# Experts of a two-block transformer on one core: gate and up as plain float32 matmuls in four column groups over 96 slots, weights unsplit

## The chip, the cores and the metric

The kernel runs on one core of a Trainium2 chip. The metric is the device time of one execution in microseconds, the median of several runs. The engines are TensorE (PE in the profile, with its weight loads as PEld), VectorE (DVE), ScalarE (ACT), GpSimd (POOL) and SyncE (SP, which issues most of the DMAs).

## What is computed

A sequence of 256 tokens with 1024 features passes through two blocks of two layers each, all in float32: mixers, feed-forward layers, and at the very end a layer of eight experts of which each token takes two. Only that last layer is touched here. From the reference:

```python
def swiglu(h, w_gate, w_up, w_down):
    return (jax.nn.silu(h @ w_gate) * (h @ w_up)) @ w_down

def moe_swiglu(h, router, w_gate, w_up, w_down):
    ...
    probs = jax.nn.softmax((ht @ router).astype(F32), axis=-1)
    top_p, top_i = lax.top_k(probs, TOP_K)
    top_p = top_p / jnp.sum(top_p, axis=-1, keepdims=True)
    gates = jnp.sum(jax.nn.one_hot(top_i, N_EXPERTS, dtype=F32) * top_p[..., None], axis=1).astype(h.dtype)
    out = jnp.zeros_like(ht)
    for e in range(N_EXPERTS):
        out = out + gates[:, e:e + 1] * swiglu(ht, w_gate[e], w_up[e], w_down[e])
    return out.reshape(B, T, D)
```

Here there are 8 experts, 2 for each token, 1024 features and 1536 features inside an expert. Gate, up and down of an expert are 6 MB each, 151 MB for the layer.

## The kernel before

**Split products.** Most products of the kernel are made of three. A weight tile W arrives as float32 in a buffer `raw` (`wload`, L294: one DMA on SP's queue, 1 MB). ScalarE copies it to `wh` (L302), VectorE subtracts to get `wl` (L303), both in the type float32r. Activations are split in the same way. `mm3` (L308) then adds three matmuls: high times high (L310), high times low (L311), low times high (L312). There are 3 buffers `raw`, and 5 each of `wh` and `wl` (1024 columns, so half a `raw` each); the experts' stage has 4 more of `raw` (`MORE["mo"]`, L33). Other products, in the mixers, are plain float32 matmuls without a split. L1279 in the hybrid mixer is one of these: it multiplies with 64 stationary columns and writes the lower and the upper half of the partitions in turn.

**The experts' stage** (`moe`, L1375). `first_up` (L1454) does gate and up of the first 512 features of expert 0 for all 256 tokens while the router works; the matmuls begun in `head_rows` at the end of the stage ahead belong to it. `router` and `shares` give each token its two experts, its place in each, and its weight. `experts(base, mid)` (L1477) then treats every expert on at most 128 tokens: those with places `base` to `base + 127`. In it:

- `places` (L1481) makes the one-hot matrices `oh`.
- `gather` (L1490) multiplies x by `oh` for two experts at a time and puts their tokens, features on partitions, into `xg`, split in two parts (L1499 on TensorE, L322 and L324 for the split).
- `up(e, b)` (L1508) makes 512 features of gate and up: 8 row tiles x 2 x 3 products, into the PSUM tag `pj`, then silu and the product `u` (L1523, L1524). There are three such blocks b for an expert.
- `turn` (L1527) transposes `u` (L1548) and splits it into `ph` and `pl`.
- `down` (L1551) multiplies by down's weights into two banks of the tag `sm`; after the third block it turns `oh` (L1568, `ohT` L1570) and splits the result into `yh`, `yl`.
- `scatter` (L1577) multiplies back to the tokens (L1584, L1585) and adds to x (L1586).

The loop at L1599 does `up` of a block, within it the turn and the scatter of earlier ones, then `down` of the block before. A second call, `experts(P, {})`, handles tokens past the 128th of an expert; it stands under a condition on the number of tokens of the fullest expert (L1629 to L1631), and each engine jumps over it when the condition is false. Except where `manual_schedule` is used, a scheduler sets the order of instructions on every engine; for TensorE in `first_up` the written order holds, in `experts` the scheduler's.

## Time and profile before

| | |
|---|---|
| median of 3 runs | 1692.63 us (1692.15 to 1693.01) |
| span of the profiled execution | 1693.5 us |
| TensorE busy in it | 1643.3 us, 97% |
| VectorE busy | 1243.0 us, 73% |
| ScalarE busy | 1025.3 us, 61% |
| moved by DMA | 334.77 MB, mean 198 GB/s |
| first product of the experts to the last down, about | 1257 to 1683 us |

The profile is one execution; the sum of an argument is made against its 1693.5 us, which are 0.9 us above the median. Busy time of TensorE counts pipelined matmuls whose ends are modelled, so the pace of a matmul is read from the starts of successive ones, not from the duration of one.

### The profile page before, as it was taken

The page shows a single profiled execution, that of the slowest core. Times are in us where ns is not written, and L with a number is a line of the kernel's source. Part 1 is how long each engine was busy: PE and PEld are TensorE (multiplying, and loading weights), DVE is VectorE, ACT ScalarE, POOL GpSimd, SP SyncE. Part 2 cuts the span into 40 slices and gives each one's busy share as a digit, 9 for nine tenths or more (in the row PEclk, how much of TensorE's full clock was granted, in tenths as well). Part 3 has the DMA queues.
Part 4 walks back from the last instruction along what each step waited for, and adds up shares of the span by engine and source line. Part 5 has one row for each costly group of instructions (what it writes and reads, how often), then busy time and mean ns, then how long its engine had stood idle before and what let it go on. Part 6 is the DMA issues. An engine that isn't in the chain of part 4 may idle for free.

```text
span 1693.5 us, 25594 instructions
## 1 busy us (share of the span) xinstructions
PE 1643.3 (97%) x9987; PEld 1451.9 (86%) x9987; DVE 1243.0 (73%) x1867; ACT 1025.3 (61%) x1610; POOL 136.0 (8%) x158
## 2 busy tenths in 40 slices
PE   7999999999999999989999999989999999999998
PEld 5878999888889998989899998989778888888886
DVE  6667877666577776886475555875589999999996
ACT  6646555555575555663364444653468777877775
POOL 2100000021000000261000001360000000000000
PEclk9999999999999999999999999999999999999999
DMA  7433555454335553440165554420459899898992
GB/s 279 150 125 127 205 193 180 169 192 167 123 129 198 194 179 137 175 144 1 50 228 195 178 183 156 162 100 1 154 203 362 323 351 353 340 349 327 348 366 111
DMA packets 47376, 334.77 MB, mean 198 GB/s; under 512 B 5424, under 2 KB 5456, under 8 KB 8720
## 3 DMA queue, kind: packets, MB, share of 16 engines
q1 hardware_dynamic: 45936, 327.70, 53.1%
q0 software_dynamic: 736, 4.29, 0.7%
q8 instruction: 80, 1.31, 0.3%
q10 hardware_dynamic: 576, 1.08, 0.2%
q14 instruction: 48, 0.39, 0.1%
HBM read 332.00 MB, written 1.05 MB: 197 GB/s over the span
## 4 chain that ended last, share of the span: by engine, by line
PE 87%; issue 5%; DVE 3%; ACT 2%; POOL 2%; DMA 0%; POOLq 0%; DVEq 0%; ACTq 0%
PE pj L312 18%; PE pj L310 18%; PE pj L311 18%; PE sm L312 7%; PE sm L310 6%; PE sm L311 6%; PE sm L421 2%; PE sm L1147 2%; PE sm L1156 2%; DVE wl L303 1%; PE sm L1150 1%; ACT wh L302 1%; PE sm L1499 1%; POOL qa L1233 1%; PE pj L1255 1%
## 5 line engine op out<-in xcount | busy, mean ns | idle before, releaser
L303 DVE TENSOR_TENSOR wl<-raw,wh 128x1024 fp32r<-128x1024 f32 (+1 forms) x632 | 755.7, 1213 | 208.3 <-ACT wh L302 200.1
L302 ACT CAST wh<-raw 128x1024 fp32r<-128x1024 f32 (+1 forms) x632 | 651.0, 1039 | 293.6 <-PE pj L312 112.6
L310 PE MATMUL pj<-hTh,wh 128*128 128x256 f32 x1192 | 336.1, 282 | 0.0
L311 PE MATMUL pj<-hTl,wh 128*128 128x256 f32 x1192 | 335.8, 282 | 0.0
L312 PE MATMUL pj<-hTh,wl 128*128 128x256 f32 x1192 | 335.3, 282 | 0.0
L310 PEld LDWEIGHTS pj<-hTh,wh 128*128 128x128 f32 x1192 | 227.1, 191 | 1.1
L311 PEld LDWEIGHTS pj<-hTl,wh 128*128 128x128 f32 x1192 | 227.2, 191 | 0.9
L312 PEld LDWEIGHTS pj<-hTh,wl 128*128 128x128 f32 x1192 | 226.8, 191 | 0.2
L311 PE MATMUL sm<-wl,ph 128*128 128x512 f32 x456 | 179.2, 393 | 0.0
L312 PE MATMUL sm<-wh,pl 128*128 128x512 f32 x456 | 177.5, 393 | 0.0
L310 PE MATMUL sm<-wh,ph 128*128 128x512 f32 x456 | 166.4, 393 | 0.5 <-ACT ph L316 0.5
L311 PE MATMUL pj<-wl,xgh 128*128 128x512 f32 x368 | 145.4, 395 | 0.8 <-DVE wl L303 0.8
L312 PE MATMUL pj<-wh,xgl 128*128 128x512 f32 x368 | 143.8, 391 | 0.0
L310 PE MATMUL pj<-wh,xgh 128*128 128x512 f32 x368 | 142.3, 391 | 0.0
L312 PE MATMUL pj<-wh,hTl 128*128 128x512 f32 (+1 forms) x368 | 138.1, 378 | 3.3 <-DVE hTl L324 3.3
L310 PE MATMUL pj<-wh,hTh 128*128 128x512 f32 (+1 forms) x368 | 139.5, 381 | 0.5 <-ACT hTh L322 0.4
L311 PE MATMUL pj<-wl,hTh 128*128 128x512 f32 (+1 forms) x368 | 137.5, 376 | 0.0
L310 PEld LDWEIGHTS sm<-wh,ph 128*128 128x128 f32 x456 | 85.7, 188 | 19.0 <-ACT ph L316 0.7
L312 PEld LDWEIGHTS sm<-wh,pl 128*128 128x128 f32 x456 | 85.5, 188 | 19.1
L311 PEld LDWEIGHTS sm<-wl,ph 128*128 128x128 f32 x456 | 85.6, 188 | 18.5
L832 DVE SCALAR_TENSOR_TENSOR u<-pj,tab_f,u 128x254 f32<-128x254 f32 (+1 forms) x176 | 82.7, 478 | 20.0 <-ACT u L830 18.2
L312 PEld LDWEIGHTS pj<-wh,hTl 128*128 128x128 f32 x368 | 69.5, 189 | 15.7 <-DVE hTl L324 6.1
(402 smaller groups left out, 2411.0 us busy)
## 6 DMA issues: line engine op xcount, KB each, us to landing
raw<-in_mo_u SPq DMA_DIRECT2D x96, 1024.0 KB, 5.2
raw<-in_mo_d SPq DMA_DIRECT2D x48, 1024.0 KB, 5.0
raw<-in_up SPq DMA_DIRECT2D x44, 1024.0 KB, 4.8
raw<-in_dn SPq DMA_DIRECT2D x22, 1024.0 KB, 4.7
raw<-in_fg_u SPq DMA_DIRECT2D x22, 1024.0 KB, 4.8
raw<-in_od_b SPq DMA_DIRECT2D x18, 1024.0 KB, 4.8
raw<-in_hy_b SPq DMA_DIRECT2D x16, 768.0 KB, 4.2
raw<-in_hy_a SPq DMA_DIRECT2D x12, 1024.0 KB, 4.7
```

What stands on the lines that cost most here:

```text
L302: A.copy(h, r)
L303: V.tensor_sub(m, r, h.bitcast(F32))
L310: T.matmul(o, lh, rh, start=first, stop=False)
L311: T.matmul(o, lh, rl, start=False, stop=False)
L312: T.matmul(o, ll, rh, start=False, stop=last)
L421: T.matmul(q, hT[j][:, k, ts_], w[f][k][v], start=t + k + i == 0, stop=k == KT - 1 and i == 2, skip_group_check=True)
L832: V.scalar_tensor_tensor(u[:, g, sh:], q[:, : S - sh], cw[:, f, g, wi : wi + 1], u[:, g, sh:], op0=OP.mult, op1=OP.add)
L1147: T.matmul(pq[:, i * P : (i + 1) * P], Am[:, i], U[:, i], start=i == 0, stop=True, skip_group_check=True)
L1150: T.transpose(pt[:, i * P : (i + 1) * P], U[:, i], ident)
L1156: T.matmul(pu[:, i * P : (i + 1) * P], Tt[:, i], Q[:, i], start=i == 0, stop=True, skip_group_check=True)
L1233: G.tensor_scalar(dst[b, h], C[b], cc[b, h : h + 1], cb[b, h : h + 1], op0=OP.mult, op1=OP.add)
L1255: T.matmul(sc, qa[:, h, ts_], ka[:, h, :w], start=e == 0, stop=False, skip_group_check=True)
```

## The change

Gate and up in `experts` no longer use split products. The gathered tokens `xg` are kept as one float32 tensor, 96 slots for each expert instead of 128, in three tiles of 32 tokens. The weights go from DRAM into seven buffers `mw` of [128, 1536] (768 KB a DMA, gate or up of one row tile) and from there straight into plain float32 matmuls: the tokens are stationary (32 columns), a quarter of the 1536 columns moves in each of four matmuls, and each of the four writes its own group of 32 partitions. Silu, product and transposes work on three tiles of [128, 384]. Down keeps its split products, with 96 stationary columns, over all 1536 features in one go after `up` of the next expert. The PSUM banks are dealt out by hand: six for gate and up and the turns, two for down, gather and scatter. The whole loop now stands under `manual_schedule` for TensorE. Tokens past the 96th and the 192nd of an expert have a conditional pass each, so there are two conditions. `xh` and `xl` move into another pool. The first 512 features of expert 0 come from an array of their own, `mo_h`, as before in content. The diff takes out comments as well, so line numbers after it are other ones.

```diff
-MORE = {"mo": (4, 0), "f": (0, 4), "sw": (0, 4), "ev": (1, 1), "od": (1, 1)}
+MORE = {"mo": (0, 0), "f": (0, 4), "sw": (0, 4), "ev": (1, 1), "od": (1, 1)}
+C32 = 32
+NT = 3
+CAP = C32 * NT
+MW_BUFS = 7
...
-                    def gather(e):
-                        xg[e // 2] = split_pair("xg")
+                    def gather(e, kind="dn"):
+                        xg[e // 2] = xgs[e // 2 % 2]
                         for k0 in range(0, KT, 2):
-                            p = ps()
+                            p = bank(kind)
...
-                            split_gain([(h[:, k0 + k], lo[:, k0 + k], p[:, k * S : (k + 1) * S],
-                                         nrm["g"][:, k0 + k : k0 + k + 1]) for k in range(2)])
+                            for k in (k0, k0 + 1):
+                                src = grp(p[:, (k - k0) * S : (k - k0 + 1) * S], 2)[:, :, :CAP]
+                                A.activation(xg[e // 2][:, k], src, AF.Copy, scale=nrm["g"][:, k : k + 1])
...
-                    def up(e, b):
...
-                                w = unit(e, b, g, half)
-                                for k in range(4):
-                                    kk = half * 4 + k
-                                    mm3(q, h[:, kk, es_], lo[:, kk, es_], *w[k], kk == 0, kk == KT - 1)
...
+                    def up(e):
+                        lo = 512 if e in mid else 0
+                        n = (DE - lo) // 4
+                        h = xg[e // 2]
+                        o = [[bank("up") for _ in range(2)] for _ in range(NT)]
+                        for k in range(KT):
+                            for m in range(2):
+                                w = sp.tile([P, DE], F32, tag="mw", name="mw", bufs=MW_BUFS)
+                                nc.sync.dma_start(w[:, : 4 * n], a["mo_u"][(e * KT + k) * 2 + m][:, lo:])
+                                for t in range(NT):
+                                    l = h[:, k, e % 2, t * C32 : (t + 1) * C32]
+                                    for g in range(4):
+                                        T.matmul(o[t][m][g * C32 : (g + 1) * C32, :n], l, w[:, g * n : (g + 1) * n],
+                                                 start=k == 0, stop=k == KT - 1, skip_group_check=True)
                             yield
+                        made[e] = []
+                        for t in range(NT):
+                            u = sp.tile([P, 384], F32, tag="u", name="u", bufs=4)
+                            A.activation(u[:, :n], o[t][0][:, :n], AF.Silu)
+                            V.tensor_mul(u[:, :n], u[:, :n], o[t][1][:, :n])
+                            made[e].append(u)
...
+                        for t, u in enumerate(made.pop(e)):
+                            p = bank("up")
+                            for i in range(c):
+                                T.transpose(p[:, i * P : (i + 1) * P], u[:, i * P : (i + 1) * P], ident)
+                            part = lambda z: z[:, k1:, t * C32 : (t + 1) * C32].rearrange("p (g c) n -> p c g n", c=c)
+                            split(part(ph), part(pl), p[:, : c * P].rearrange("p (c g n) -> p c g n", c=c, g=4))
...
+                            mm3(acc[n][:CAP], ph[:, kk], pl[:, kk], w[kk][0][:, c], w[kk][1][:, c], kk == 0, kk == nk - 1)
...
+                    for e in range(NE):
+                        side = iter(())
+                        if e >= 2:
+                            side = scatter(e - 2)
+                        if e % 2 == 1 and e + 1 < NE:
+                            side = chain(side, gather(e + 1))
+                        for k, _ in enumerate(up(e)):
+                            if k % 2 == 1:
+                                next(side, 0)
+                                next(side, 0)
+                        rest(side)
+                        if e:
+                            rest(down(e - 1))
+                        turn(e)
+                    last = down(NE - 1)
+                    next(last)
+                    rest(scatter(NE - 2, "up"))
+                    rest(last)
+                    rest(scatter(NE - 1, "up"))
...
-                experts(0, mid)
+                banks["up"] = ([ps("pj") for _ in range(4)] + [ps() for _ in range(2)], 0)
+                banks["dn"] = ([ps() for _ in range(2)], 0)
+                xgs = [xp.tile([P, KT, 2, CAP], F32, tag=tag, name="xg", bufs=2) for tag in ("xTh", "xTl")]
+                with tc.manual_schedule(engines=MAN):
+                    experts(0, mid)
                 full = nc.values_load(mosti[:1, :1], min_val=0, max_val=S)
-                with tc.If(full > P):
-                    experts(P, {})
+                for base in (CAP, 2 * CAP):
+                    with tc.If(full > base):
+                        with tc.manual_schedule(engines=MAN):
+                            experts(base, {})
```

Three places of the order, as it stands before and after. In the rows, a name ahead of the arrow is what is written, those behind it are read, and x4 is a count.

TensorE, in the middle of the stage before, where gather, scatter and `up` of one expert meet (`xgh`, `xgl` are the split tokens, `yh` and `yl` the split result of the expert before):

```order
L1499 MATMUL sm<-oh,xl 128x256
L310 MATMUL pj<-wh,xgh 128x512
L1584 MATMUL sm<-yh,ohT 128x512
L1585 MATMUL sm<-yl,ohT 128x512
L311 MATMUL pj<-wl,xgh 128x512
L312 MATMUL pj<-wh,xgl 128x512
```

After, from the end of down(0) over the turn of expert 1 into up(2) and to its first scatter (L1532 are the matmuls in column groups, 4 of them a bundle):

```order
L316 MATMUL sm<-wh,pl 96x512
L1587 MATMUL pj<-tab_com,oh 96x128 x2
L1566 MATMUL sm<-tab_com,u 128x128 x6
L1566 MATMUL pj<-tab_com,u 128x128 x3
L1532 MATMUL pj<-mw,xg 32x384 x8
L1532 MATMUL sm<-mw,xg 32x384 x4
...
L1532 MATMUL pj<-mw,xg 32x384 x4
L1603 MATMUL sm<-yh,ohT 128x512
L1604 MATMUL sm<-yl,ohT 128x512
```

Single products of gather and scatter stood among those of gate and up; now they stand in blocks between runs of L1532, and down, turn and the next up follow one another.

ScalarE, the same stretch before:

```order
L316 CAST ph<-sm 128x512
L1570 CAST ohT<-sm 128x256
L302 CAST wh<-raw 128x1024 x3
L1523 ACTIVATE u<-pj 128x512
L302 CAST wh<-raw 128x1024 x8
L316 CAST yh<-sm 128x512 x2
L302 CAST wh<-raw 128x1024
```

And after (`ph` comes in three pieces, one for each tile of tokens):

```order
L1538 ACTIVATE u<-sm 128x384
L306 CAST wh<-raw 128x1024 x11
L320 CAST yh<-sm 96x512 x2
L1589 CAST ohT<-pj 96x256
L320 CAST ph<-pj 128x3x4x32 x2
L306 CAST wh<-raw 128x1024
L320 CAST ph<-sm 128x3x4x32
```

The casts of weights are fewer and stand in one block behind the silu; the last piece of `ph` stands behind one more of them. VectorE's order (`yl`, `pl`, `wl`) goes the same way.

SyncE, the loads around the reading of the fullest expert's count (`mosti`), before:

```order
L1629 TENSOR_LOAD mosti
L1629 ISA x2
L297 DMA raw<-in_mo_u 128x2048 x3
L297 DMA raw<-in_mo_d 128x2048 x2
L297 DMA raw<-in_mo_u 128x2048 x4
```

And after:

```order
L1650 TENSOR_LOAD mosti
L1650 ISA x2
L301 DMA raw<-in_mo_d 128x2048 x2
L1528 DMA mw<-in_mo_u 128x1024 x9
L1528 DMA mw<-in_mo_u 128x1536 x23
L301 DMA raw<-in_mo_d 128x2048 x6
L1528 DMA mw<-in_mo_u 128x1536 x16
```

Units of down came after every four of gate and up; now they come six in a row after sixteen pieces, and seven pieces of the next expert's gate and up stand ahead of them.

## Rows read from the trace of the kernel before

**Rows 1.** Page, part 1: engine, busy us, share of the span, instructions

```profile
PE 1643.3 (97%) x9987; PEld 1451.9 (86%) x9987; DVE 1243.0 (73%) x1867; ACT 1025.3 (61%) x1610; POOL 136.0 (8%) x158
```

**Rows 2.** Windows: start:end, busy us PE PEld DVE ACT POOL, clock, DMA, GB/s

```profile
1262.00:1676.00 414.00, 414.00 (x1909) 341.35 (x1907) 385.07 (x388) 325.48 (x368) 0.00 (x0) 1.00 0.88 333
...
1410.00:1420.00 10.00, 10.00 (x45) 8.14 (x45) 9.21 (x9) 8.12 (x9) 0.00 (x0) 1.00 1.00 392
```

**Rows 3.** Waits, 1260 to 1693 us: waiter, releaser, total us, times, longest

```profile
ACT wh L302 <- PE pj L312: 40.9, 99, 2.5
ACT wh L302 <- PE sm L312: 35.2, 72, 2.9
```

**Rows 4.** Groups by form, 1260 to 1693 us: count, busy us, mean ns, idle

```profile
L303 DVE TENSOR_TENSOR wl<-raw,wh 128x1024 fp32r<-128x1024 f32 x275 | 327.2, 1220 | 28.0 <-ACT wh L302 21.9 <-PE pj L312 1.6
L302 ACT CAST wh<-raw 128x1024 fp32r<-128x1024 f32 x275 | 286.5, 1053 | 77.7 <-PE pj L312 40.9 <-PE sm L312 35.2 <-DVE wl L303 1.2
...
L312 PE MATMUL pj<-wh,xgl 128*128 128x512 f32 x367 | 143.3, 391 | 0.0
...
L312 PE MATMUL sm<-wh,pl 128*128 128x512 f32 x192 | 75.5, 395 | 0.0
```

**Rows 5.** Timeline, PE, the first products of two successive gathers: start, us, what

```profile
1325.01 0.28 PE L1499 MATMUL sm<-oh,xh 128*128 128x256 f32 x1
...
1434.88 0.28 PE L1499 MATMUL sm<-oh,xh 128*128 128x256 f32 x1
```

**Rows 6.** Timeline, PE, inside a down, ten products apart

```profile
1398.12 0.39 PE L310 MATMUL sm<-wh,ph 128*128 128x512 f32 x1
...
1400.45 0.40 PE L312 MATMUL sm<-wh,pl 128*128 128x512 f32 x1
```

**Rows 7.** Timeline, PE, the end of the first gather and what follows

```profile
1255.96 0.28 PE L1499 MATMUL sm<-oh,xh 128*128 128x256 f32 x1
...
1256.89 0.39 PE L310 MATMUL pj<-wh,xgh 128*128 128x512 f32 x1
...
1258.56 0.50 PE L311 MATMUL pj<-wl,xgh 128*128 128x512 f32 x1 [0.81 <-DVE wl L303]
```

**Rows 8.** Timeline, PE, plain float32 of 128 columns, and L1279 in two column groups

```profile
788.87 0.83 PE L1147 MATMUL sm<-U,Am 128*128 128x128 f32 x6
789.54 0.49 PE L1150 MATMUL sm<-tab_com,U 128*128 128x128 f32 x3
789.97 0.66 PE L1279 MATMUL pj<-wT,vf 128*64 128x128 f32 x8
790.56 0.70 PE L1255 MATMUL pj<-ka,qa 128*128 128x256 f32 x2
791.10 0.22 PE L1256 MATMUL pj<-causb,identb 128*128 128x128 bf16 x1
```

**Rows 9.** Timeline, PE, plain float32 of 256 columns

```profile
749.09 1.03 PE L1106 MATMUL sm<-C,tab_hy 128*128 128x256 f32 x4
749.96 1.24 PE L1114 MATMUL sm<-kq,kz 128*128 128x256 f32 x5
```

**Rows 10.** Timeline, PE, the last turn and the last down

```profile
1676.67 0.38 PE L1568 MATMUL sm<-tab_com,oh 128*128 128x128 f32 x2
1677.50 0.50 PE L310 MATMUL sm<-wh,ph 128*128 128x512 f32 x1 [0.46 <-ACT ph L316]
```

**Rows 11.** Timeline, DVE, the second product of gate and up

```profile
1256.69 0.68 DVE L1473 TENSOR_TENSOR u<-u,pj 128x512 f32<-128x512 f32 x1
```

**Rows 12.** The line of the condition: count, ns min/median/max, first and last start

```profile
L1630 SPq EVENT_SEMAPHORE  x8: 17/17/17, 1690.1 to 1691.8; - x8
...
L1630 DVEq COMPARE_BRANCH  x1: 72/72/72, 1686.9 to 1686.9; - x1
L1630 SPq COMPARE_BRANCH  x1: 50/50/50, 1687.1 to 1687.1; - x1
...
L1630 DVEq EVENT_SEMAPHORE  x1: 21/21/21, 1690.5 to 1690.5; - x1
```

More of the change, by code (lines that the diff above doesn't have):

```diff
@@ L1458, in first_up @@
                     o[0, 0], o[0, 1] = yield from head
-                    w = [unit(0, 0, 1, half) for half in range(2)]
+                    w = [wload(a["mo_h"][2 + half], 4, 512) for half in range(2)]
                     for t in range(2):
@@ L1474, in first_up, with bank @@
                         split(uh[:, t], ul[:, t], u)
-                    mid[0, 0] = (uh, ul)
+                    mid[0] = (uh, ul)
+                banks = {}
+                def bank(kind):
+                    b, at = banks[kind]
+                    banks[kind] = (b, (at + 1) % len(b))
+                    return b[at]
                 def experts(base, mid):
@@ L1534, in turn @@
+                    def turn(e):
+                        ph = sp.tile([P, DE // P, CAP], F32R, tag="ph", name="ph", bufs=2)
+                        pl = sp.tile([P, DE // P, CAP], F32R, tag="pl", name="pl", bufs=2)
+                        turned[e] = (ph, pl)
+                        k1 = 0
+                        if e in mid:
+                            k1 = 4
+                            u = mid[e]
                             for k0 in (0, 2):
-                                p = ps()
+                                p = bank("up")
@@ L1559, in down @@
+                    def down(e):
+                        ph, pl = turned.pop(e)
+                        acc = [bank("dn"), bank("dn")]
+                        nk = DE // P
+                        w = [None] * nk
+                        steps = [(kk, n) for kk in range(nk) for n in range(2)]
+                        if e == NE - 1:
+                            steps = steps[: 2 * nk - 8] + [(kk, n) for n in range(2) for kk in range(nk - 4, nk)]
                         for kk, n in steps:
                             if w[kk] is None:
-                                w[kk : kk + 2] = wload(a["mo_d"][(e * 3 + b) * 2 + kk // 2], 2, D)
+                                w[kk : kk + 2] = wload(a["mo_d"][e * nk // 2 + kk // 2], 2, D)
@@ L1577, in scatter @@
-                    def scatter(e):
+                            mm3(acc[n][:CAP], ph[:, kk], pl[:, kk], w[kk][0][:, c], w[kk][1][:, c], kk == 0, kk == nk - 1)
+                            if (kk, n) == (3, 1):
+                                yield
+                        p = bank("up")
+                        for t in range(2):
+                            T.transpose(p[:CAP, t * P : (t + 1) * P], oh[:, t, e, :CAP].bitcast(F32), ident)
+                        ohT = sp.tile([P, 2, P], F32R, tag="ohT", name="ohT", bufs=2)
@@ L1579, in scatter @@
+                        A.copy(ohT[:CAP], p[:CAP, :S].rearrange("p (t n) -> p t n", t=2))
+                        yh = sp.tile([P, 2, 512], F32R, tag="yh", name="yh", bufs=1)
+                        yl = sp.tile([P, 2, 512], F32R, tag="yl", name="yl", bufs=1)
+                        for n in range(2):
+                            split(yh[:CAP, n], yl[:CAP, n], acc[n][:CAP])
+                        back[e] = (ohT, yh, yl)
+                    def scatter(e, kind="dn"):
                         ohT, yh, yl = back.pop(e)
@@ L1589, in scatter @@
                                     (nc.sync, nc.scalar)[t].dma_start(out[t][:, c], x[:, t, c])
[L1591 removed]
+                                yield
+                    rest(gather(0, "up"))
                     for e in range(2, NE):
                         places(e)
[L1594 to L1615 removed]
+                    for e in range(NE):
[17 more added lines that the diff above has]
+                    rest(scatter(NE - 1, "up"))
                 mid = {}
```

100 lines of the change are left out of this document (17 added, 83 removed).

## The prediction

> **What bounds the kernel now.** I read the page's first part, then the stretch in which the experts run, by windows, then the waits there, then the order of single matmuls. The page has TensorE busy for 97% of the span [rows 1]. The experts take the last quarter: from 1262 to 1676 us TensorE is busy for all 414 us, VectorE for 385, ScalarE for 325, and the DMA engines carry 333 GB/s at a share of 0.88 [rows 2]. Three resources are near full, so the waits decide: ScalarE's casts wait 76 us for matmuls to free a buffer [rows 3], and TensorE hardly waits at all. The stage goes at TensorE's pace; what VectorE and ScalarE do for the weights (275 casts and 275 subtractions [rows 4]) lies beside it. Freeing those two engines gains nothing by itself. The sum has to be made on TensorE.
>
> **Before, per expert.** Two experts take 1434.88 - 1325.01 = 109.87 us, from one gather to the next [rows 5]. In them are 144 matmuls of down at 0.233 us (ten in 2.33 us [rows 6]), 33.6 us; 32 of the gather at 0.117 us (eight in 0.93 us [rows 7]), 3.7; 16 of the scatter at 0.23, 3.7; 28 transposes of 128 columns at 0.11, 3.1. The other 65.8 us are the 288 of gate and up: 0.229 us each, small waits included, 33.0 us for one expert.
>
> **Gate and up after.** A plain float32 matmul stands in the trace as two records, each at half the pace of the split ones: 128 columns go at 0.112 us (six in 0.67 us [rows 8]), 256 at 0.2175 (four in 0.87 us [rows 9]). The straight line through both gives 0.323 us for 384 columns. An expert has 16 weight tiles x 3 tiles of tokens x 2 records = 96 steps of four column groups. If the four go side by side, that is 96 x 0.323 = 31.0 us; if one after the other, 124 us. The change rests on this, and the kernel has a small case of it: L1279 writes two groups of 64 columns, and its eight records take 0.59 us from the first to the next line's start [rows 8], where 8 x 0.112 = 0.89 us would be needed in a row. With the 0.1 us or so that entering and leaving costs (below), two groups go side by side in full. I take that for four. So 31.0 - 33.0 = -2.0 us for each of seven experts, **-14.0**. Expert 0 has two thirds of the columns: 96 x 0.2175 = 20.9 against 96 x 0.229 = 22.0, **-1.1**.
>
> TensorE's arithmetic is thus nearly the same before and after: three split products over 128 slots against four passes over 96. The gain is small enough that the small terms decide.
>
> **Entering and leaving column groups.** From L1150 at 789.54 to the end of the first two L1255 at 791.10 are 1.56 us [rows 8]; the paces give 3 x 0.11 + 4 x 0.112 + 2 x 0.2175 = 1.21. So a run in column groups pays 0.35 us for getting in and out. The new order has 24 such runs (one for expert 0, three to four for each other, since scatter and gather steps interrupt them): at most 8.5 us; where an entry meets a wait it is hidden, so **+8.0**, bounds 4 and 8.5.
>
> **Down, turn, side work.** Down keeps its 576 matmuls, with 96 instead of 128 stationary columns. I allow 0 to -2.3 us (0.229 instead of 0.233 us, the pace of gate and up) and take **-1.2**. There are 69 transposes of u instead of 92: 23 x 0.11, **-2.5**. Gather and scatter keep their counts.
>
> **Waits that are new.** (a) After down of e-1 the engines write three things in a row: yh and yl, ohT, then ph and pl of three tiles, with one cast and subtraction of a weight ahead of the third pl (the order of ScalarE above). With 1.05 and 1.22 us for these [rows 4] and about 0.5 for a 384-column piece (an estimate: 0.40 and 0.46 by columns from the same rows, and something fixed), the third pl is done 4.9 us after down's end. Behind it stands the third tile's second product of up(e+1), since both share a bank. TensorE gets there after 1.2 us of turning and five steps of 0.65: at 4.5. So 0.4 us six times, 2.4; the gather that ends up(3) and up(5) holds the banks of down for 0.4 each, 0.8; the first turn has no down ahead of it and waits 0.8. Together **+4.0**, bounds 1 and 8. (b) The last turn goes straight into the last down, which needs all three pieces: 4.9 - 1.7 = 3.2 us of waiting, where now 0.6 us pass (from the end of the two L1568 to 1677.50 [rows 10]): **+2.6**. (c) The first gather now takes banks of the products pj. Its fourth group must wait for the multiplication of L1473, which ends at 1257.37 (1256.69 + 0.68 [rows 11]), and ends 0.94 later, at 1258.3; now the first product stands at 1256.89, with 0.8 us of waiting soon behind it [rows 7]: **+0.6**. (d) There are two conditional passes instead of one. Jumping over one takes 3.0 us on SP (1687.1 to 1690.1) and 3.6 on VectorE (1686.9 to 1690.5) [rows 12]; with a second, VectorE is through at 1694.1, where all other work of today is done at 1691.8: **+2.3**, bounds 0 and 3.6. Nobody hides it, it is the end of the program.
>
> **Weights.** Gate and up come in pieces of 768 KB, seven buffers, no cast; down in 1 MB as before. SP's order puts seven pieces of the next up ahead of down's units, and the fifth and sixth unit of a down wait for casts that ScalarE begins only when up has ended. I followed the buffers through one expert: the sixth unit goes out about 21 us after down begins, the nine pieces behind it are needed from 32 us on. An expert's 18.9 MB must come in 54.4 us, 347 GB/s. At a share of 1.00 the queue did 392 [rows 2], and 333 at 0.88 is 378 at full share. So the transfers keep up with some 4 us to spare for each expert, and I take **0**.
>
> **Sum:** -14.0 - 1.1 + 8.0 - 1.2 - 2.5 + 4.0 + 2.6 + 0.6 + 2.3 = -1.3 us on the profiled span of 1693.5, 1692.2. That span lies 0.9 us above the median of 1692.63, so I forecast **1691.3 us**: no change beyond 0.2% (3.4 us, about what a measurement of this kernel can tell from none). With the bounds of the terms its own range is 1684 to 1700.
>
> **Rivals.**
> (1) **Four groups don't go side by side in full.** The trace shows two groups of 64, never four of 32, and four must read four streams of float32 at once. The experts' column work is 7 x 31.0 + 20.9 = 238 us. If only three streams' worth gets through, it grows by a third, +79: 1770 us; if two, 1929. It decides from a step of 0.331 us on: 8 ns more, over 672 steps, is the 5 us that make it slower by 0.2%. Against it speaks that the second group of L1279 cost nothing measurable. The Trainium skill, page "TensorE: Matmul & The Clock Gate", section "Part 3: Packing small matmuls", gives 2.38 times the speed for three column tiles, not three. No run here shows three. By that ratio carried over (0.79 of full) the column work would take 238/0.79 = 301 us, an estimate from that page, and the kernel 1754.
> (2) **The weights arrive late.** If what the stage does now, 333 GB/s [rows 2], were all that these pieces reach, an expert takes 56.7 us instead of 54.4: 7 x 2.3 = +16, 1707 us. For it speaks that the spare is only 4 us of 54; against it, the 392.
> (3) **Entering and leaving is cheap.** If 32-column weights load under the running group and the six waits of (a) close up, 7 of the 8 us and 3 of the 4 us go: 1681 us, faster. For it speaks that I took the price of a full drain from a 64-column case.
> (4) **The change does extra passes.** More than 96 tokens on one expert would run a second pass of some 400 us. Counted from the reference on its inputs the fullest expert has 74, so this is all but excluded.
>
> **How the numbers follow.** Forecast 0.60, rival 1 0.08, rival 2 0.10, rival 3 0.20, rival 4 and the like 0.02. Of the forecast's 0.60, a third lies below 1689.2 and a sixth above 1696. Faster: 0.20 + 0.20 = 0.40; slower: 0.10 + 0.08 + 0.10 + 0.02 = 0.30; within 0.2%: 0.30. The single likeliest time stays 1691.3. The range reaches down through rival 3 and up to rival 2's time, 1679 to 1706; outside are rival 1, rival 4 and the tails.
>
> **What the changed profile would show.** Records of the new line 32 columns wide: starts in bundles of four, 0.323 us from bundle to bundle (0.43 or more if rival 1 is right); a gap of 0.2 us or so at each change between them and other lines; TensorE's waits no longer near zero but 8 to 12 us, most for pl and ph after each down; VectorE and ScalarE busy for less than 60% of the stage; SP waiting for TensorE, not for VectorE. If TensorE's waits name a DMA, rival 2 is right. If bundles come at 0.323 and the time is still far off, the small terms of this sum were wrong.

## The result, and the profile after

| | before | after |
|---|---|---|
| median | 1692.82 us (4 runs, 1692.15 to 1693.01) | 1709.35 us (4 runs, 1707.29 to 1710.83) |
| ratio | | 1.0097 (95% interval 1.0083 to 1.0112) |
| span of the profiled execution | 1693.5 us | 1708.3 us |
| first product of gate and up of expert 0 that is in `experts` | 1256.89 us | 1257.23 us |
| end of the last matmul | 1685.7 us | 1695.5 us |

The change makes the kernel slower by 1.0%, 14.8 us on the profiled spans. The forecast was 1691.3 with a range of 1679 to 1706. Of the 14.8 us, 9.5 lie between the first product and the last matmul, and 5.0 behind the last matmul (7.8 us before, 12.8 after).

By windows, the experts' stage of the changed kernel (it answers [rows 2]; the columns are the same):

```profile
1257.00:1693.00 436.00, 420.25 (x3904) 222.21 (x3902) 162.42 (x186) 134.36 (x192) 0.00 (x0) 0.99 0.86 320
```

VectorE and ScalarE are down from 93% and 79% of the stage to 37% and 31% (162 and 134 of 436 us). Their busy time is not what sets the time of the stage. TensorE, busy without a gap in [rows 2], now stands for 16 us of the stage.

The waits of the changed kernel from 1250 us on (waiter, releaser, us in total, times, longest; [rows 3] shows two rows of before):

```profile
ACT wh L306 <- PE sm L316: 36.1, 41, 4.0
ACT wh L306 <- DMA raw<-in_mo_d: 21.9, 18, 3.0
...
PE pj L1532 <- DVE pl L321: 4.8, 4, 1.5
...
PE pj L1532 <- ACT ohT L1589: 3.3, 3, 1.3
PE sm L314 <- ACT ph L320: 3.2, 1, 3.2
PE sm L1532 <- DVE pl L321: 3.0, 2, 1.5
```

Before, ScalarE's casts of weights waited 76.1 us in all for matmuls to free a buffer [rows 3], and the waits there name no DMA. Now 18 of them wait 21.9 us for a DMA of down's weights, and TensorE waits for pl, ohT and ph. SP's queue, from 1200 us on:

```profile
SPq L301 <- DVE wl L307: 177.2, 50, 17.1
```

The loads of down's weights wait until a subtraction has freed one of the three buffers `raw`.

**The arithmetic is as fast as forecast.** TensorE behind the turn of expert 1, going into gate and up of expert 2. Eight records are two bundles of four column groups:

```profile
1333.05 0.38 PE L1587 MATMUL pj<-tab_com,oh 128*96 128x128 f32 x2
...
1334.34 0.85 PE L1532 MATMUL pj<-mw,xg 128*32 128x384 f32 x8
1336.48 0.85 PE L1532 MATMUL pj<-mw,xg 128*32 128x384 f32 x8 [1.28 <-ACT ohT L1589]
1338.82 0.85 PE L1532 MATMUL sm<-mw,xg 128*32 128x384 f32 x8 [1.49 <-DVE pl L321]
1339.49 0.83 PE L1532 MATMUL pj<-mw,xg 128*32 128x384 f32 x8
1340.13 0.83 PE L1532 MATMUL sm<-mw,xg 128*32 128x384 f32 x8
1340.78 2.12 PE L1532 MATMUL pj<-mw,xg 128*32 128x384 f32 x24
```

From 1339.49 to 1340.13 to 1340.78 it is 0.645 us for two bundles, 0.323 for one: what one stream alone would need. The four go side by side in full. A run of 24 bundles takes 7.88 us where nothing disturbs it; this one, from 1334.34 to the scatter at 1345.40, takes 11.07. The two gaps, 1.28 and 1.49 us, stand at its second and third pair of bundles. ScalarE and VectorE in the same place:

```profile
1327.65 2.00 ACT L306 CAST wh<-raw 128x1024 fp32r<-128x1024 f32 x2 [3.04 <-DMA raw<-in_mo_d]
1330.13 2.00 ACT L306 CAST wh<-raw 128x1024 fp32r<-128x1024 f32 x2 [0.49 <-DMA raw<-in_mo_d]
1333.20 1.99 ACT L306 CAST wh<-raw 128x1024 fp32r<-128x1024 f32 x2 [1.06 <-DMA raw<-in_mo_d]
1335.10 1.05 ACT L320 CAST yh<-sm 96x512 fp32r<-96x512 f32 x2
1336.05 0.37 ACT L1589 CAST ohT<-pj 96x256 fp32r<-96x256 f32 x1
1336.32 0.86 ACT L320 CAST ph<-sm 128x384 fp32r<-128x384 f32 x2
1337.06 1.07 ACT L306 CAST wh<-raw 128x1024 fp32r<-128x1024 f32 x1
1338.00 0.50 ACT L320 CAST ph<-pj 128x384 fp32r<-128x384 f32 x1
```

```profile
1334.28 2.36 DVE L307 TENSOR_TENSOR wl<-raw,wh 128x1024 fp32r<-128x1024 f32 x2 [0.70 <-ACT wh L306]
1336.56 1.28 DVE L321 TENSOR_TENSOR yl<-sm,yh 96x512 fp32r<-96x512 f32 x2
1337.75 1.01 DVE L321 TENSOR_TENSOR pl<-sm,ph 128x384 fp32r<-128x384 f32 x2
```

Down ends at 1333.05. The casts at 1330.13 and 1333.20 are for the next expert's down, which begins 38 us later (1371.15), and they wait for their transfers. Everything that TensorE needs stands behind them: yh, ohT, ph on ScalarE, and yl and pl on VectorE. ohT is written 3.0 us behind the start of its matmuls and ends the first gap; the second pl is done at 1338.8 and ends the second.

The first run behind each turn takes 11.07, 10.55, 8.95, 12.76, 9.01 and 9.80 us. Less 7.88 each, that is **14.8 us** lost. How late ScalarE begins with yh says where they go:

| turn of expert | 1 | 2 | 3 | 4 | 5 | 6 |
|---|---|---|---|---|---|---|
| yh begins behind down's end, us | 2.05 | 1.53 | -0.06 | 2.06 | -0.01 | 0.79 |
| lost in the run behind it, us | 3.18 | 2.67 | 1.07 | 4.88 | 1.13 | 1.92 |

Each turn loses 1.1 us and, on top, what yh is late. Only the fourth loses more, 1.7 us, because TensorE's clock falls there (last section). So of the 14.8 us some 6.4 are late casts, 6.6 are the chain behind a yh that begins on time, and 1.7 are the clock.

**The last down** has the same chain ahead of it and no other work to put between:

```profile
1667.40 0.49 PE L1566 MATMUL pj<-tab_com,u 128*128 128x128 f32 x3
1671.06 0.47 PE L314 MATMUL sm<-wh,ph 128*96 128x512 f32 x1 [3.17 <-ACT ph L320]
...
1672.93 0.74 PE L316 MATMUL sm<-wh,pl 128*96 128x512 f32 x1 [1.17 <-DVE pl L321]
1673.46 0.63 PE L314 MATMUL sm<-wh,ph 128*96 128x512 f32 x1
```

The granted clock there, by windows:

```profile
1673.00:1675.60 2.60, 2.60 (x7) 1.70 (x7) 0.00 (x0) 0.62 (x1) 0.00 (x0) 0.50 0.08 32
```

From the first product that turns `oh` (1666.53) to the end of down's first 24 matmuls (1679.37) it is 12.84 us; without waits it would be 0.22 + 1.08 + 24 x 0.232 = 6.9. Of the 6.0 us, 4.3 are the two waits and some 1.4 the clock: behind the waits TensorE was granted 0.50, its lower level of 1.2 GHz, and its matmuls stand 0.43 us apart (from 1672.93 to 1675.91 seven steps take 2.98 us instead of 1.62). Before, the same place lost 0.6 [rows 10].

**The end.** The line of the conditions, from the source view (it answers [rows 12]: count, ns min/median/max, first and last start), before and after:

```profile
L1630 ACTq EVENT_SEMAPHORE  x1: 17/17/17, 1691.4 to 1691.4; - x1
```

```profile
L1652 DVEq COMPARE_BRANCH  x2: 56/64/72, 1696.6 to 1700.2; - x2
...
L1652 ACTq COMPARE_BRANCH  x2: 45/50/54, 1698.5 to 1702.6; - x2
L1652 DVEq EVENT_SEMAPHORE  x2: 21/21/21, 1700.1 to 1704.4; - x2
L1652 ACTq EVENT_SEMAPHORE  x2: 17/17/17, 1702.5 to 1705.9; - x2
```

On VectorE the first jump goes from 1696.6 to 1700.1 and the second from 1700.2 to 1704.4. ScalarE is through last: it issues two transfers of the output first (from 1695.63 on), comes to its first jump at 1698.5 and leaves the second at 1705.9. That is 10.4 us behind the last matmul; before it was 5.7 (1691.4).

### The profile page after: what moved, and what is told of

It reads as the page before. It is cut to its first block, busy times and chain, and to the rows that moved or that the text cites. A ratio compares the mean times of both kernels' runs of the same rounds, so it can differ in the third digit from the quotient of the medians.

```text
span 1708.3 us, 28919 instructions
## 1 busy us (share of the span) xinstructions
PE 1636.6 (96%) x11932; PEld 1323.4 (77%) x11932; DVE 1014.3 (59%) x1653; ACT 830.2 (49%) x1428; POOL 135.8 (8%) x158
## 3 DMA queue, kind: packets, MB, share of 16 engines
q10 hardware_dynamic: 576, 1.08, 0.2%
## 4 chain that ended last, share of the span: by engine, by line
PE 81%; DVE 5%; issue 5%; ACT 3%; DMA 3%; POOL 2%; DVEq 0%; ACTq 0%; POOLq 0%
PE pj L316 13%; PE pj L315 13%; PE pj L314 13%; PE pj L1532 9%; PE sm L314 5%; PE sm L316 5%; PE sm L315 5%; PE sm L1532 5%; DVE wl L307 2%; DMA raw<-in_mo_d 2%; PE sm L425 2%; PE sm L1151 2%; PE sm L1160 2%; ACT wh L306 1%; PE sm L1154 1%
## 5 line engine op out<-in xcount | busy, mean ns | idle before, releaser
L307 DVE TENSOR_TENSOR wl<-raw,wh 128x1024 fp32r<-128x1024 f32 (+2 forms) x448 | 538.1, 1212 | 228.5 <-ACT wh L306 224.4
L306 ACT CAST wh<-raw 128x1024 fp32r<-128x1024 f32 (+2 forms) x448 | 458.9, 1033 | 277.2 <-PE pj L315 102.2
L1532 PE MATMUL pj<-mw,xg 128*32 128x384 f32 (+1 forms) x2048 | 183.7, 475 | 8.1 <-DVE pl L321 4.8
L314 PE MATMUL sm<-wh,ph 128*128 128x512 f32 (+1 forms) x456 | 179.7, 394 | 3.2 <-ACT ph L320 3.2
L315 PE MATMUL sm<-wl,ph 128*128 128x512 f32 (+1 forms) x456 | 179.3, 393 | 0.0
L316 PE MATMUL sm<-wh,pl 128*128 128x512 f32 (+1 forms) x456 | 177.8, 393 | 1.2 <-DVE pl L321 1.2
L1532 PEld LDWEIGHTS pj<-mw,xg 128*32 128x32 f32 x2048 | 64.3, 110 | 100.9 <-issue 81.3
L1532 PE MATMUL sm<-mw,xg 128*32 128x384 f32 (+1 forms) x1024 | 102.3, 478 | 3.0 <-DVE pl L321 3.0
L314 PEld LDWEIGHTS sm<-wh,ph 128*128 128x128 f32 (+1 forms) x456 | 80.8, 177 | 30.4 <-issue 3.4
L316 PEld LDWEIGHTS sm<-wh,pl 128*128 128x128 f32 (+1 forms) x456 | 80.8, 177 | 25.5 <-DVE pl L321 1.6
L315 PEld LDWEIGHTS sm<-wl,ph 128*128 128x128 f32 (+1 forms) x456 | 80.7, 177 | 22.6
```

Of the source, the lines that this page charges most:

```text
L306: A.copy(h, r)
L307: V.tensor_sub(m, r, h.bitcast(F32))
L314: T.matmul(o, lh, rh, start=first, stop=False)
L315: T.matmul(o, lh, rl, start=False, stop=False)
L316: T.matmul(o, ll, rh, start=False, stop=last)
L1532: T.matmul(o[t][m][g * C32 : (g + 1) * C32, :n], l, w[:, g * n : (g + 1) * n], start=k == 0, stop=k == KT - 1, skip_group_check=True)
```

## Experiments

Theory A: in the changed kernel the pieces that TensorE waits for stand in two in-order queues behind casts of weights whose transfers are late. Theory B: the weights are simply late, and TensorE would wait wherever the turn stands. Theory C: the chain from the turn to pl is too long in itself. Each kernel below was timed beside the kernel before on the same chip (1692.35 to 1692.52 us there).

### The turn in the middle of down

```diff
-                        if e:
-                            rest(down(e - 1))
-                        turn(e)
+                        ahead = down(e - 1) if e else iter(())
+                        next(ahead, 0)
+                        turn(e)
+                        rest(ahead)
```

> The changed kernel with one thing moved: the turn of expert e stands after the first 24 matmuls of down(e-1) instead of behind all 72. Theory A (in the changed kernel the casts that make ph and pl stand in the queues of ScalarE and VectorE behind casts of the next down's weights, which wait for their transfers; TensorE runs into the pieces' banks, 14.8 us over six experts, and once more 5 us at the last down): ph and pl are done long before down ends, so some 15 of these 20 us go (what is left is the wait for the bank of ohT), the span falls from 1708 to about 1693. Theory B (the weights are simply late, the wait sits there by chance): TensorE waits the same 15 to 20 us at another place, for mw or wh, and the span stays at 1703 to 1708.

1691.2 us (1689.4 to 1693.8), ratio 0.9992 (0.9982 to 1.0001); span 1688.3. Its waits, and TensorE from the end of a down into the next run:

```profile
ACT wh L306 <- DMA raw<-in_mo_d: 16.5, 15, 2.4
```

```profile
1333.02 0.38 PE L1587 MATMUL pj<-tab_com,oh 128*96 128x128 f32 x2
1333.34 1.50 PE L1532 MATMUL pj<-mw,xg 128*32 128x384 f32 x16
```

The casts still wait for transfers, 16.5 us in all, and TensorE goes on without a gap: the six runs together take 0.2 us more than 7.88 each. From the first product to the end of the last matmul the stage takes 419.3 us instead of 438.3, and the median is 18 us lower. Between the last two downs TensorE still waits 1.5 us, for the two banks that both use. B is out: at TensorE's own pace the weights are not late.

### Gate and up's pieces loaded once

```diff
-                                w = sp.tile([P, DE], F32, tag="mw", name="mw", bufs=MW_BUFS)
-                                nc.sync.dma_start(...)
+                                if len(keep) < MW_BUFS:
+                                    keep.append(sp.tile([P, DE], F32, tag=f"mw{len(keep)}", name="mw", bufs=1))
+                                    nc.sync.dma_start(keep[-1], a["mo_u"][(e * KT + k) * 2 + m])
+                                w = keep[(k * 2 + m) % MW_BUFS]
```

> Leaves out most of the weight traffic: the pieces of gate and up are loaded once, the first seven, and used again for every other piece, so DMA carries only down's weights in the stage (the results are other ones). The orders of TensorE, ScalarE and VectorE are the changed kernel's. Theory A1 (the casts are late because transfers are): no cast waits for a transfer, the casts run at the pace at which TensorE frees wh, and the first run behind each turn waits about 0.4 us as forecast: six waits of 2 to 3 us in all instead of 14.8; span about 1693. Theory A2 (ScalarE and VectorE are too slow in this order whatever the transfers do): the waits stay at 10 to 15 us, span about 1705.

1700.84 us (one run), span 1699.1. The six runs lose 0.77, 2.35, 0.89, 1.00, 0.93 and 0.86: 6.8 us, where 14.8 were. The same place as above:

```profile
1333.81 0.38 PE L1589 MATMUL pj<-tab_com,oh 128*96 128x128 f32 x2
...
1335.11 1.50 PE L1534 MATMUL pj<-mw,xg 128*32 128x384 f32 x16
1337.17 0.85 PE L1534 MATMUL sm<-mw,xg 128*32 128x384 f32 x8 [0.56 <-DVE pl L321]
```

A1 expected 2 to 3 us and A2 10 to 15; it is about midway between the two. ScalarE's casts still wait 15.5 us for transfers, most of them 0.7 at a time; there are three buffers `raw` as before. But at five of the six turns they are through when down ends: here yh begins at 1333.58, ahead of down's end at 1333.81, where in the changed kernel it began 2 us behind it. At the second turn yh begins 1.2 us late, behind a cast that waited 2.2 us for its transfer, and that is the one that loses 2.35. So 8 of the 14.8 us go with the late casts. About 1 us at each turn is left, and the row shows where: at the third pair of bundles, 2.06 us behind the run's start, not at the sixth.

### One conditional pass

```diff
-                for base in (CAP, 2 * CAP):
+                for base in (CAP,):
```

> The changed kernel with one conditional pass instead of two (the pass for tokens past the 192nd is left out). By the sum of the prediction the second jump costs 2.3 us; by the trace of the changed kernel it is about 5 (12.8 us from the last matmul to the end, 7.8 before). So 1707 against 1704 us.

1705.62 us (1698.97 to 1707.67), ratio 1.0069 (1.0043 to 1.0095). The runs lie 9 us apart, so the time alone doesn't price the jump. The trace does: 6.7 us from the last matmul to the end of the span instead of 12.8.

The stage itself is the changed kernel's, so it shows the turns a second time: they lose 1.45, 4.79, 0.72, 1.06, 0.99 and 4.16 us, 13.2 in all, with yh 0.32, 1.96, -0.24, -0.08, -0.14 and 1.58 us behind down's end. The fourth turn, the worst above, is on time here. How late a cast is belongs to the execution, not to the place; what a late one costs is the same as above, and at the two worst the clock fell again.

### Five buffers raw, five mw

```diff
-MORE = {"mo": (0, 0), ...}
+MORE = {"mo": (2, 0), ...}
-MW_BUFS = 7
+MW_BUFS = 5
```

> The changed kernel with five buffers raw and five buffers mw instead of three and seven. If the casts are late because three buffers are too few to cover the time from issue to landing, they come on time and the waits behind the turns fall from 14.8 to 3 to 6 us: 1698. If they are late because the queue is full (share 0.93 over the stage), the wait stays or moves to mw: 1706 to 1712.

1706.39 us (1704.91 to 1707.99), ratio 1.0077 (1.0060 to 1.0094). The waits on TensorE:

```profile
PE pj L1532 <- DVE pl L321: 6.0, 4, 1.5
...
PE sm L1532 <- DVE pl L321: 3.0, 2, 1.5
...
PE sm L1532 <- DMA mw<-in_mo_u: 1.5, 2, 1.3
```

No cast waits for a DMA any more: at the same bytes, five buffers bring down's weights in time where three don't. So the queue's rate is not what makes them late. But the six turns now lose 1.85 us each, 11.1 in all, and alike. yh begins at 1334.15, ahead of down's end (1334.38), as it should. Yet the scheduler has put the twelfth cast between yh and ohT, where the changed kernel has it behind two pieces of ph. On ScalarE it runs from 1335.10 and ohT from 1336.05, and VectorE's order goes the same way. The expected 3 to 6 us are missed for that reason: a cast in time, but in the wrong place, costs a microsecond as well. The last line is new: with five buffers `mw` instead of seven TensorE waits for gate and up's pieces in expert 0, whose run takes 23.05 us instead of 20.86. That gives back 2.2 of the 3.7 us gained at the turns.

### The casts behind the pieces

```diff
-                                w[kk : kk + 2] = wload(a["mo_d"][e * nk // 2 + kk // 2], 2, D)
+                                w[kk : kk + 2] = early.pop((e, kk), None) or wload(a["mo_d"][e * nk // 2 + kk // 2], 2, D)
...
+                    early = {}
...
+                    def ahead(e):
+                        for kk in (0, 2):
+                            early[e, kk] = wload(a["mo_d"][(e * DE // P + kk) // 2], 2, D)
...
                         turn(e)
+                        ahead(e)
...
-                with tc.manual_schedule(engines=MAN):
+                with tc.manual_schedule(engines=MAN | {mybir.EngineType.Activation, mybir.EngineType.DVE}):
                     experts(0, mid)
```

> The turn stays behind down, as in the changed kernel. Changed is the order of ScalarE and VectorE in the experts, which is now as written: eight casts of a down, then ohT, yh and ph, and the four casts of the next down's first two units behind them (SyncE's order follows: those two units go out between pieces of gate and up). Theory A (casts ahead of ph in an in-order queue make the waits): the six waits behind the turns fall from 14.8 to 1 to 4 us, near the forecast's 2.4, and the last turn waits 3 us instead of 6: span 1693 to 1697. Theory C (it is only the slack of 11 us that the moved turn gave, the chain from turn to pl is too long wherever the casts stand): the waits stay at 10 to 15 us, 1705 to 1709.

1705.09 us (1704.37 to 1706.21), ratio 1.0075 (1.0059 to 1.0090); span 1703.5. ScalarE at the turn of expert 1:

```profile
1331.48 0.37 ACT L1589 CAST ohT<-pj 96x256 fp32r<-96x256 f32 x1 [3.74 <-PE pj L1587]
1331.75 1.07 ACT L320 CAST yh<-sm 96x512 fp32r<-96x512 f32 x2
1332.70 0.88 ACT L320 CAST ph<-sm 128x384 fp32r<-128x384 f32 x2
1333.44 0.51 ACT L320 CAST ph<-pj 128x384 fp32r<-128x384 f32 x1
1333.82 3.92 ACT L306 CAST wh<-raw 128x1024 fp32r<-128x1024 f32 x4
```

ohT, now ahead of yh, is written 0.4 us behind the start of its matmuls, the pieces follow, the casts come last. All six runs now take 8.86 us: 6 x 0.98 = 5.9 us lost instead of 14.8, more than A's 1 to 4 and well below C's 10 to 15. From the first product to the last turn the stage takes 400.6 us (1255.24 to 1655.80) against 409.5 (1257.23 to 1666.74). The gain is given back at the end. The written order brings the last down's casts late, too: its 72 matmuls and the eight of the scatter between take 26.7 us (1659.47 to 1686.13), 5.4 more than the changed kernel's (1671.06 to 1692.31, 21.25), with waits for `wh` and `wl` in them. So the span is 6.5 us above the upper end of what A gave. At the turns the casts made what A says, 9 of the 14.8 us, and C holds for the last 1 us of each.

### The conditions nested

The second condition stands inside the first, so both passes are still there for inputs that need them. Beside it the turn is in the middle, as above.

```diff
-                for base in (CAP, 2 * CAP):
-                    with tc.If(full > base):
+                with tc.If(full > CAP):
...
+                    with tc.If(full > 2 * CAP):
```

> The turn in the middle of down, as in the run above, and the second condition put inside the first, so that one jump passes over both passes. The one-condition run had 6.7 us from the last matmul to the end of the span instead of 12.8, so some 5 to 6 us go: span 1682 to 1684, time about 1685.5, faster than the kernel before by 0.4%. If the jumps run beside something else, as the forecast's 2.3 us assumed, 1688.5.

1686.92 us (1686.13 to 1690.33), ratio 0.9970 (0.9958 to 0.9982): faster than the kernel before, and than the turn in the middle alone (0.9992). From the last matmul to the end it is 7.9 us (1679.44 to 1687.39) against 12.7 with the two conditions in a row (1675.54 to 1688.26). The second jump costs 4.8 us. With the pass left out (above) it was 6.1; most of the difference lies behind ScalarE's queue, from which it is 2.2 us to the end here and 1.1 there.

### More runs in column groups, and fewer

```diff
-                            if k % 2 == 1:
-                                next(side, 0)
-                                next(side, 0)
+                            next(side, 0)
```

> The kernel of the run above with one step of gather or scatter behind every row tile instead of two behind every second: 42 runs in column groups instead of 24. By the forecast's 0.35 us for getting in and out, 6.3 us more than that run; by the trace of the changed kernel (0.09 before a run, 0.12 at its end, 0.10 in the first product behind it) 0.31 us each, 5.6 more; if the trace only shows ends that are modelled and the switch is cheap, 0 to 2 more.

1692.25 us (1691.3 to 1694.2). From the first product to the last matmul's end: 425.25 us (1257.77 to 1683.02) with 42 runs, 420.36 (1259.08 to 1679.44) with 24. The latter has 1.2 us of waits behind two turns that the former hasn't, so 6.1 us for 18 runs, 0.34 for each.

```diff
-                            if k % 2 == 1:
-                                next(side, 0)
-                                next(side, 0)
+                            if k == 1:
+                                rest(side)
```

> The opposite: all steps of gather and scatter in one block behind the second row tile, 15 runs in column groups instead of 24. By 0.31 us each 2.8 us less than with 24; against it, the blocks now wait for their two banks of PSUM (a scatter step is 0.46 us on TensorE and 0.74 on VectorE, which adds about 0.3 us for each of the last two steps: six blocks, up to 4 us). Between -3 and +2 against the run with 24.

1689.55 us (1687.78 to 1692.35), 2.6 more than with 24 runs, just above the expected -3 to +2: 421.85 us from first product to last matmul. Nine entries less would be 3.1 us, and the eight products of a scatter now take 2.89 us in one block against 2 x 1.13 in two: they wait for the two banks.

### Scatter and gather inside down

```diff
-                            if (kk, n) == (3, 1):
+                            if n == 1 and (e < NE - 1 or kk == 3):
                                 yield
...
-                        for k, _ in enumerate(up(e)):
-                            if k % 2 == 1:
-                                next(side, 0)
-                                next(side, 0)
-                        rest(side)
-                        ahead = down(e - 1) if e else iter(())
-                        next(ahead, 0)
-                        turn(e)
-                        rest(ahead)
+                        rest(up(e))
+                        for k, _ in enumerate(down(e - 1) if e else range(4)):
+                            if k == 3:
+                                turn(e)
+                            elif e:
+                                next(side, 0)
+                        rest(side)
```

> Turn in the middle of down and conditions nested, as in the fast run, and the steps of scatter and gather moved out of gate and up into down, between groups of six of its matmuls, where TensorE is not in column groups: 8 runs in column groups instead of 24. At 0.33 us for each (the run with 42 against the one with 24) 5.3 us less: span 1682, time 1682 to 1683. Against it: the scatter's four additions, 0.75 us each on VectorE, and the gather's eight copies on ScalarE now fall into down, where both engines prepare down's weights; if the weights come late by that, TensorE waits inside down, up to 1 us for each expert, and the time stays at 1686 to 1690.

The steps of scatter and gather also take banks of gate and up here. 1680.36 us (1679.45 to 1682.06), ratio 0.9930 (0.9916 to 0.9943). The stage takes 413.76 us (1256.78 to 1670.54), 6.6 less than with 24 runs; without the waits behind the turns of either run (1.2 and 0.2) it is 5.6 for 16 entries, 0.35 each. TensorE does not wait inside these downs.

```diff
-                        acc = [bank("dn"), bank("dn")]
+                        acc = [bank("up" if e == NE - 1 else "dn") for _ in range(2)]
...
-                    rest(scatter(NE - 2, "up"))
+                    rest(scatter(NE - 2))
```

> The same with the last down in two banks of gate and up instead of the two that the down ahead of it still holds. In the run with the turn in the middle TensorE stands 1.7 us between the last two downs for these banks; that goes: 1.7 us less than the run before it here, or nothing if the next thing that the last down waits for (weights) is as late.

1679.56 us (1679.10 to 1680.69), ratio 0.9925 (0.9911 to 0.9938). Span 1677.2 against 1678.5: most of the 1.7 us comes back in the scatter inside the last down, which now waits for the banks instead. Against the run ahead of it this is within the spread; against the kernel before, the two are the fastest here, by 0.7%. TensorE where a run ends and a scatter step stands inside down:

```profile
1363.00 0.83 PE L1532 MATMUL sm<-mw,xg 128*32 128x384 f32 x8
1363.76 0.47 PE L314 MATMUL sm<-wh,ph 128*96 128x512 f32 x1
...
1365.22 0.39 PE L1603 MATMUL sm<-yh,ohT 96*128 96x512 f32 x1
1365.45 0.39 PE L1604 MATMUL sm<-yl,ohT 96*128 96x512 f32 x1
1365.68 0.40 PE L314 MATMUL sm<-wh,ph 128*96 128x512 f32 x1
```

The scatter's products at 1365.22 and 1365.45 stand 0.23 us apart among down's, with nothing lost.

## Why the prediction was wrong, point by point

The forecast was 1691.3, within 0.2% of before; it came out 16.5 us above the time before. The sum on the span was -1.3 and it should have been +14.8.

| term | forecast | measured |
|---|---|---|
| gate and up, experts 1 to 7 | -14.0 | -14.0 (a bundle 0.323 us) |
| expert 0 | -1.1 | -1.1 (20.86 us) |
| entering and leaving | +8.0 | +8.2 (24 x 0.34) |
| down with 96 columns | -1.2 | about -0.7 (72 in 16.68 us, entering left out) |
| transposes | -2.5 | -2.5 |
| (a) behind six turns | +2.4 | +14.8 |
| (a) gather, first turn | +1.6 | +0.5 |
| (b) last turn to last down | +2.6 | +5.4 |
| (c) first gather | +0.6 | +0.9 (5.40 us instead of 3.74, less the 0.8 behind it) |
| (d) second jump | +2.3 | +5.0 |
| weights | 0 | 0 on TensorE itself |
| sum | -1.3 | +16.5 (span: +14.8) |

The measured terms add up to 1.7 us more than the spans differ. Of that, 1.3 lie ahead of the stage: the first gather begins at 1251.83 instead of 1253.15. Between the profiled executions of the kernels here, alike up to that place, this start differs by 4 us (1250.78 to 1254.80), so 1.3 is within that spread. The other 0.4 was not found.

- **Right:** what bounds the kernel, the pace of four column groups, the price of entering and leaving (0.35 us was read off a case of two groups of 64; 0.34 and 0.35 came out of 42, 24 and 8 runs of 32; the upper bound of 24 runs is 8.4, not 8.5, which changes nothing), that freeing VectorE and ScalarE gains nothing by itself, that the small terms decide. The Trainium skill, page "TensorEngine Tiling (Array Packing)", section "Key Properties", says that a change of the tiling mode drains TensorE, without a price; these three kernels give it for this case.
- **The step that failed, "(a) After down of e-1 the engines write three things in a row ... the third pl is done 4.9 us after down's end".** It let ScalarE and VectorE begin with yh when down ends. In the trace that holds at two of the six turns. At the other four they begin 0.8 to 2.1 us later, because casts for the next down stand ahead of yh and wait for their transfers. The order of ScalarE ahead of the prediction shows them, eleven casts ahead of yh, of which the last four are for the next down; I priced only the one behind. 8 to 9 of the 14.8 us are this, the fall of the clock behind the longest waits included (14.8 against 6.8 with most transfers taken away, and against 5.9 with the casts behind).
- **The step "Weights ... I take 0"** asked only whether TensorE gets its weights in time, and it does. It didn't ask who else waits when a transfer is late by 1 to 3 us: a cast, and with it all that is queued behind on its engine. The first line of the diff takes four buffers `raw` away from this stage (seven become three), and I gave that no price. With five, no cast waits. The prediction's signs had SP wait for TensorE and not for VectorE; it waits 177.2 us for VectorE's subtractions, which are what frees these three buffers.
- **The bank that is met first.** Without late casts a turn still loses 1 us, not 0.4. I looked for the third tile's second product, at the sixth place, and put pl at 4.9 us behind down's end. With the loads cut that was right (the third piece was done at 1338.72, 4.9 us behind 1333.81). But the third tile's first product shares its bank with the second piece, and TensorE is there after two pairs of bundles, at 1336.4, where the piece is done at 1337.1. A rotation of six banks has to be followed for every product, not for the last.
- **(b)** is the same chain with nothing between: 3.2 us forecast, 3.2 + 1.2 waited, and the clock fell on top. yh began 1.1 us late here too, and the third pl was done 6.3 us behind down's end (1672.87 against 1666.53) instead of 4.9; with five buffers `raw`, where yh is on time, it was 4.85.
- **(d)** counted VectorE's jump alone and let it end at 1694.1 where other work ended at 1691.8. The second jump is not shorter (4.2 us on VectorE), and the queue that is through last is ScalarE's, which I did not look at: it comes to its jumps 1.9 us later than VectorE and leaves them at 1705.9. The upper bound of 3.6 was too small: 4.8 by nesting.
- **The rivals.** (1), four groups not in full, is out: a bundle takes 0.323 us. The Trainium skill, page "TensorE: Matmul & The Clock Gate", section "Part 3: Packing small matmuls", has 2.38 times for three column tiles; carried over as in the prediction that is 0.41 us, an estimate from that page, and the trace does not agree. (2), late weights, was nearest in time (1707), which is luck, and half right in cause: late, yes, but not by rate, and never at TensorE itself. (3) is out, the price is there. (4) did not occur. The rival that was missing is a queue: a load that nobody needs yet, standing ahead of a result that TensorE is about to need.

Two things stay open. What a turn loses (1.1 to 4.9 us) follows from how late its casts are and from the clock, but why a transfer is late in one execution and not in another was not taken apart; with five buffers `raw`, where no cast waits for a transfer, the turns are alike. And the order in which the scheduler puts the casts of two downs was replaced by hand in one way only.

## What to carry to other kernels

When a change cuts buffers of a stream, ask not only whether the engine at the end still gets its data, but what stands behind each waiting instruction in its own queue: a prefetch that may be late belongs behind the results that the bottleneck waits for, or the results are made earlier, as here in the middle of down. Where PSUM banks rotate by hand, follow the rotation product by product to the first that meets a bank still being read. Put work that leaves a tiling mode next to work that has left it anyway, and count every jump over a pass that is not taken, on the slowest queue.

## What the hardware showed that I had not expected

- The second of two jumps over passes that are not taken cost 4.8 us at the end of the program, more than the first takes on VectorE (3.5 us). The Trainium skill, page "Runtime: NRT & Kernel Launch", section "Instruction fetch mechanics", says that a taken branch to a target outside the window that has been fetched must fetch it first. The rows above agree with that (3.5 and 4.2 us on VectorE between the branch and the next instruction), though they don't show a fetch itself; the compare-and-branch is 56 to 72 ns there.
- In the changed kernel's stage TensorE's clock fell to its lower level behind waits of 1.2 to 3.2 us, in two places. One is the last down above. In the other, two waits of 1.30 and 1.49 us came 2.3 us apart, and six bundles took 3.64 us (1505.07 to 1508.71) instead of 1.94:

```profile
1502.73 0.85 PE L1532 MATMUL pj<-mw,xg 128*32 128x384 f32 x8 [1.30 <-ACT ohT L1589]
1505.07 1.51 PE L1532 MATMUL sm<-mw,xg 128*32 128x384 f32 x8 [1.49 <-DVE pl L321]
```

The granted clock behind them, by windows:

```profile
1505.00:1507.00 2.00, 1.93 (x14) 0.60 (x17) 1.62 (x3) 0.00 (x0) 0.00 (x0) 0.52 0.99 410
1507.00:1509.00 2.00, 2.00 (x20) 0.70 (x16) 0.00 (x0) 0.00 (x0) 0.00 (x0) 0.62 0.65 165
```

It was 0.52 and 0.62 on average, so mostly 1.2 GHz, the lower of its two levels. Behind waits of the same length in the expert shown above (1.28 and 1.49 us) it stayed at 1.00. In the run with one conditional pass it fell behind waits of 0.81 and 1.49 us (0.54 from 1615 to 1617 us), which are shorter. So the price of a short wait is not its length alone, and what decides it these runs don't tell.
